# Output projections of an fp32 two-layer trunk: both token parts in one 512-column product, and the last down-projection token-major

## The chip, the cores and the metric

The kernel runs on one core of a Trainium2 chip. The metric is the device time of one execution in microseconds (us). Three runs of the kernel before gave 625.13, 625.70 and 626.88 us, median 625.7 us. The trace was taken on one further, profiled execution: its span, from the first to the last instruction, is 622.1 us.

## The reference

A batch of one, 256 tokens (S) of 1024 features (D), two layers, all float32. Layer 0 mixes tokens by attention, layer 1 by a gated short convolution; each is followed by a SwiGLU feed-forward with 2816 hidden features (D_FF). A conditioning vector c gives six rows of 1024 values for each layer (shift, scale and gate for the mixer, shift, scale and gate for the feed-forward):

```python
sc = jax.nn.silu(c)
for i in range(DEPTH):
    mod = sc @ w_ada[i] + b_ada[i]
    sh_m, sc_m, g_m, sh_f, sc_f, g_f = jnp.split(mod, 6, axis=-1)
    h = modulate(x, norm_mix[i], sh_m, sc_m)          # rmsnorm(x) * (1 + scale) + shift
    if i % N_MIXERS == 0:
        y = moba_attention(h, w_qkv[j], w_o[j], q_gain[j], k_gain[j])
    else:
        y = short_conv(h, w_in[j], conv_w[j], w_out[j])
    x = x + g_m[:, None, :] * y
    h = modulate(x, norm_ffn[i], sh_f, sc_f)
    x = x + g_f[:, None, :] * swiglu(h, w_gate_up[i], w_down[i])
return x
```

With 256 tokens there is one attention block, so the attention is plain causal attention in 8 heads of 128.

## The kernel before

**Products in parts.** A float32 operand is split into a high and a low part in TensorE's faster float32r format, and a product is three passes: high by high, high by low, low by high (mm3, L285 to L289). One pass is one TensorE instruction with a 128x128 stationary operand and 256 moving columns. A new stationary operand is loaded for each pass (the rows of PEld).

**Layout.** The residual x is held feature-major (xT: 128 features on the partitions, 8 tiles k, 256 tokens along). In most products the weights are stationary and the 256 tokens move, so that the result is feature-major again.

**The weight stream.** Weights and adaLN pieces come in chunks of up to 1 MB, all issued on SP's queue (load, L82 to L86) in the order of their use, into five buffers. A weight chunk (wf) is split into wh on ScalarE (L98) and wl on VectorE (L99), in two halves, into three buffers each. An adaLN piece (wa) is multiplied and summed on VectorE (L114, L116). A chunk's buffer is free again, and the next load can be issued, when its last reader on VectorE is done. What VectorE and ScalarE do, and in which order, is set by a scheduler that fills each engine's list from the order in which the program asks for the chunks (get, produce).

**Output projections.** out_proj (L406 to L431) does w_o of the attention (tiles op_o), w_out of the convolution (op_co), and w_down of both layers (op_d). It makes 2 tiles of 128 output features out of a column block of 256, over 8 k-steps for w_o and w_out and 22 for w_down: 64, 64, 176 and 176 steps (tile, k) of three passes. At the end of a tile, residual (L404) adds gate times product to xT in one VectorE instruction, and Norm.take prepares the next norm: a square and a scaled high part on ScalarE (L359, L373), the low part on VectorE (L374), a sum of squares on POOL (L364, L367). At its fifth tile (k == 4) it also writes the shift columns (L380, L381).

**After an output projection** comes raw_gemm (L437): the first two chunks of the next layer part are multiplied with the un-normed x (tiles raw_f, raw_m), and the norm's own sums over partitions (ms_n, L387 and L388) run in their midst, with POOL's sum and the last tile's square as operands.

**The last gate.** The gate of layer 1's feed-forward (part 5 of its adaLN) is summed over the partitions as 24 one-column bf16 products (mod_ps, L151) of three bf16 parts (L126, L127), right ahead of the last down-projection.

**The end.** store (L826 to L836) turns each finished tile of xT back to tokens: two 128x128 transposes by ident into out_ps (L828), a copy on ScalarE (L832), and a DMA on SP (L834, L836). The first six tiles' transposes run between products of the last down-projection, those of the last two after it.

## Time and profile before

| | us |
|---|---|
| three runs, median (lowest to highest) | 625.7 (625.13 to 626.88) |
| profiled execution: span, first to last instruction | 622.1 |
| profiled execution: its own time | not given beside the span; the median lies 3.6 above the span |
| PE busy | 609.7 (98%) |
| PEld busy | 595.8 (96%) |
| DVE busy | 473.6 (76%) |
| ACT busy | 323.1 (52%) |
| DMA moved | 156.07 MB, mean 251 GB/s |
| TensorE's granted clock over the span | 0.999 of full speed |

PE is TensorE's products, PEld its weight loads, DVE VectorE, ACT ScalarE, POOL GpSimd, SP SyncE (which issues the DMAs). Products overlap in the array, and a product's end is modelled, so a row's duration is longer than what the product costs. What one costs in a row of products is the distance from its start to the start of the next. Lines (L289) are lines of the kernel.

### The profile page before, as it was taken

Reading aid. Unit: us, or ns where it says so; the run is one execution under the profiler, and the core shown is the slowest. Engines: PE = TensorE matmul, PEld = TensorE weight load, DVE = VectorE, ACT = ScalarE, POOL = GpSimd, SP = SyncE. Lnnn points to the kernel's source line nnn. Section 1 sums busy time; section 2 is a strip of 40 time slices with the busy share of each in tenths; the row PEclk is TensorE's granted clock in tenths of the full one; section 3 lists DMA queues with packets and bytes.
Section 4 is the critical chain, followed back from the end, with each engine's and each line's share of the span. In section 5 each row is a group of like instructions: output and inputs, shape, how many; then the busy total and the mean of one; then the engine's idle time right before and its main releaser. Section 6 shows DMA issues by size and latency. Waiting matters only on the chain.

```text
span 622.1 us, 12512 instructions
## 1 busy us (share of the span) xinstructions
PE 609.7 (98%) x5291; PEld 595.8 (96%) x5291; DVE 473.6 (76%) x668; ACT 323.1 (52%) x518; POOL 19.2 (3%) x26
## 2 busy tenths in 40 slices
PE   7999999999999999999999999999999999999997
PEld 5789999999999999999999999998999999999997
DVE  5567999989989899979888989658976467644440
ACT  5335977466655455535355745545744435533330
POOL 0000000020000000000110000012000000000000
PEclk9999999999999999999999999999999999999999
DMA  9999999966699999798998497646388677655200
GB/s 271 329 331 354 385 370 335 303 219 223 210 323 322 347 333 335 257 318 303 319 302 278 133 304 241 210 138 205 108 299 271 201 225 235 204 188 178 94 18 17
DMA packets 127455, 156.07 MB, mean 251 GB/s; under 512 B 2822, under 2 KB 114856, under 8 KB 127400
## 3 DMA queue, kind: packets, MB, share of 16 engines
q1 hardware_dynamic: 127400, 155.28, 75.6%
q8 instruction: 41, 0.67, 0.5%
q14 instruction: 14, 0.11, 0.1%
HBM read 154.22 MB, written 1.05 MB: 250 GB/s over the span
## 4 chain that ended last, share of the span: by engine, by line
PE 88%; DMA 3%; DVE 3%; issue 3%; ACT 1%; SPq 0%; POOLq 0%; POOL 0%; ACTq 0%
PE pu L289 7%; PE pu L288 7%; PE op_d L287 7%; PE pu L287 7%; PE op_d L289 7%; PE op_d L288 7%; PE pg L289 6%; PE pg L288 6%; PE pg L287 6%; DMA wa<-in_w_ada_dram 2%; DMA wf_qk<-in_w_qkv_dram 1%; PE pv L287 1%; PE pb L288 1%; PE pv L289 1%; PE pb L287 1%
## 5 line engine op out<-in xcount | busy, mean ns | idle before, releaser
L116 DVE SCALAR_TENSOR_TENSOR acc<-wa,sc,acc 128x1024 f32<-128x1024 f32 x70 | 89.8, 1283 | 8.8 <-DMA wa<-in_w_ada_dram 7.5
L98 ACT ACTIVATE wh_d<-wf_d 128x1024 fp32r<-128x1024 f32 (+1 forms) x48 | 45.5, 981 | 69.7 <-issue 47.2
L99 DVE TENSOR_TENSOR wl_d<-wf_d,wh_d 128x1024 fp32r<-128x1024 f32 (+1 forms) x48 | 53.6, 1144 | 30.7 <-ACT wh_d L98 30.5
L98 ACT ACTIVATE wh_u<-wf_u 128x1024 fp32r<-128x1024 f32 x44 | 44.3, 1051 | 45.3 <-issue 34.5
L98 ACT ACTIVATE wh_g<-wf_g 128x1024 fp32r<-128x1024 f32 x44 | 45.5, 1050 | 40.7 <-issue 40.7
L99 DVE TENSOR_TENSOR wl_u<-wf_u,wh_u 128x1024 fp32r<-128x1024 f32 x44 | 52.7, 1233 | 14.0 <-ACT wh_u L98 14.0
L99 DVE TENSOR_TENSOR wl_g<-wf_g,wh_g 128x1024 fp32r<-128x1024 f32 x44 | 54.5, 1245 | 2.1 <-ACT wh_g L98 2.0
L287 PE MATMUL op_d<-a1h,wh_d 128*128 128x256 f32 x176 | 50.3, 286 | 0.0
L287 PE MATMUL op_d<-a0h,wh_d 128*128 128x256 f32 x176 | 50.2, 285 | 0.0
L289 PE MATMUL op_d<-a1h,wl_d 128*128 128x256 f32 x176 | 50.0, 284 | 0.0
L289 PE MATMUL op_d<-a0h,wl_d 128*128 128x256 f32 x176 | 50.0, 284 | 0.0
L288 PE MATMUL op_d<-a1l,wh_d 128*128 128x256 f32 x176 | 49.6, 282 | 0.0
L288 PE MATMUL op_d<-a0l,wh_d 128*128 128x256 f32 x176 | 49.5, 281 | 0.0
L289 PE MATMUL pg<-f1h,wl_g 128*128 128x256 f32 x160 | 44.8, 280 | 0.0
L289 PE MATMUL pu<-f1h,wl_u 128*128 128x256 f32 x160 | 44.8, 280 | 0.0
L287 PE MATMUL pg<-f1h,wh_g 128*128 128x256 f32 x160 | 44.6, 279 | 0.0
L288 PE MATMUL pg<-f1l,wh_g 128*128 128x256 f32 x160 | 44.6, 279 | 0.0
L287 PE MATMUL pu<-f1h,wh_u 128*128 128x256 f32 x160 | 44.6, 279 | 0.0
L288 PE MATMUL pu<-f1l,wh_u 128*128 128x256 f32 x160 | 44.6, 279 | 0.0
L287 PE MATMUL pg<-f0h,wh_g 128*128 128x256 f32 x160 | 44.5, 278 | 0.0
L289 PE MATMUL pg<-f0h,wl_g 128*128 128x256 f32 x160 | 44.4, 278 | 0.0
L289 PE MATMUL pu<-f0h,wl_u 128*128 128x256 f32 x160 | 44.4, 278 | 0.0
(315 smaller groups left out, 2103.6 us busy)
## 6 DMA issues: line engine op xcount, KB each, us to landing
wa<-in_w_ada_dram SPq DMA_DIRECT2D x40, 1024.0 KB, 6.1
wf_g<-in_w_gate_up_dram SPq DMA_DIRECT2D x22, 1024.0 KB, 6.6
wf_u<-in_w_gate_up_dram SPq DMA_DIRECT2D x22, 1024.0 KB, 7.5
wf_d<-in_w_down_dram SPq DMA_DIRECT2D x16, 1024.0 KB, 6.3
wa<-in_w_ada_dram SPq DMA_DIRECT2D x16, 512.0 KB, 7.1
wf_d<-in_w_down_dram SPq DMA_DIRECT2D x8, 768.0 KB, 5.7
wf_qk<-in_w_qkv_dram SPq DMA_DIRECT2D x8, 512.0 KB, 8.1
wf_v<-in_w_qkv_dram SPq DMA_DIRECT2D x4, 1024.0 KB, 7.5
```

The lines of the kernel that those rows point to most:

```text
L98: nc.scalar.activation(wh[:, a:b], wf[:, a:b], AF.Copy)
L99: nc.vector.tensor_sub(wl[:, a:b], wf[:, a:b], wh[:, a:b].bitcast(F32))
L116: nc.vector.scalar_tensor_tensor(acc, w[:, kk], sc[:, k:k + 1], acc, op0=ALU.mult, op1=ALU.add)
L287: nc.tensor.matmul(ps, ah, bh, start=first, stop=False, skip_group_check=True)
L288: nc.tensor.matmul(ps, ah, bl, start=False, stop=False, skip_group_check=True)
L289: nc.tensor.matmul(ps, al, bh, start=False, stop=last, skip_group_check=True)
```

## The change

1. **Pairs are one tile.** new_pair and wide_pair return one tile [128, 2, nk, 256] with the high part at index 0 and the low part at 1, so that both parts of one k lie in one access pattern.
2. **Output projections** of w_o, w_out and layer 0's w_down use mm512 in place of mm3: one product of 512 moving columns (the weight's high part by [high, low]) and one of 256 (the weight's low part by high), into the two halves of a PSUM tile of 512 columns. A step (tile, k) has two instructions where it had three; the moving columns stay 768. residual adds the two halves in two VectorE instructions where it was one: 24 more of 128x256 in all, 8 at each of the three.
3. **The last down-projection** is token-major (tok_wide, project): 128 tokens of an activation are stationary and 512 weight columns move. Its chunks are 4 k-steps of 512 columns (rows of 2 KB) where they were 8 of 256. 264 products of 512 columns stand where 528 of 256 stood. The end is a multiplication by the gate and an addition of x on VectorE for each of four 128x512 results, and a DMA.
4. **The last gate as rows.** b_ada's row is read broadcast into 128 partitions by a DMA on SP, and gate_rows adds the sum over partitions, by two float32 products of 512 columns, in place of the 24 bf16 ones and the making of their parts.
5. **x to tokens early.** The transposes of x (16 of 128x128, and 4 copies on ScalarE) are made in layer 1's feed-forward, after its second to fifth pair of chunks (to_tokens), where 16 of the result stood in and after the last down-projection.

The core of the diff:

```diff
     def new_pair(tag, name, nk):
-        return (act.tile([P, nk, S], F32R, tag=tag + "h", name=name + "h"),
-                act.tile([P, nk, S], F32R, tag=tag + "l", name=name + "l"))
+        return act.tile([P, 2, nk, S], F32R, tag=tag, name=name)
...
+    def mm512(ps, lhs, both, first, last):
+
+        ah, al = lhs
+        nc.tensor.matmul(ps, ah, both, start=first, stop=False, skip_group_check=True)
+        nc.tensor.matmul(ps[:, 1], al, both[:, 0], start=False, stop=last, skip_group_check=True)
+
     def residual(ps, l, gate, k):
-        nc.vector.scalar_tensor_tensor(xT[:, k], ps, mcol(l, gate, k), xT[:, k], op0=ALU.mult, op1=ALU.add)
+        for n in range(2):
+            nc.vector.scalar_tensor_tensor(xT[:, k], ps[:, n], mcol(l, gate, k), xT[:, k], op0=ALU.mult, op1=ALU.add)
...
-                    mm3(pss[j, o], (wh[:, k, cs], wl[:, k, cs]), (xs[0][:, base + k], xs[1][:, base + k]),
-                        base + k == 0, base + k == total - 1)
+                    mm512(pss[j, o], (wh[:, k, cs], wl[:, k, cs]), xs[:, :, base + k],
+                          base + k == 0, base + k == total - 1)
...
+    def gate_rows(acc):
+
+        for n in range(2):
+            cs = slice(n * 2 * CW, (n + 1) * 2 * CW)
+            ps = ps_misc(f"gate_ps_{n}")
+            nc.tensor.matmul(ps, one.to_broadcast([P, P]), acc[:, cs], start=True, stop=True)
+            nc.vector.tensor_add(last["gate"][:, cs], last["gate"][:, cs], ps)
...
+    WIDE = 2 * CW
+    DOWN = ((0, 4), (4, 4), (8, 4), (12, 4), (16, 4), (20, 2))
...
+        if l == DEPTH - 1:
+            for j in range(2):
+                for i, (a, n) in enumerate(DOWN):
+                    dn.append(w(("d", l, j, i), w_down[l][a * P:(a + n) * P, j * WIDE:(j + 1) * WIDE], n))
+            return gu, dn
...
+    def tok_wide(pss, keys, xs, between={}, final=False):
+
+        total, base = sum(nk for _, nk in keys), 0
+        for i, (key, nk) in enumerate(keys):
+            wh, wl = get(key)
+            steps = [(k, t) for k in range(nk) for t in range(2)]
+            if final and i == len(keys) - 1:
+                steps.sort(key=lambda s: s[1])
+            seen = set()
+            for k, t in steps:
+                if k not in seen:
+                    seen.add(k)
+                    for fn, *args in between.get(base + k, ()):
+                        fn(*args)
+                ts = slice(t * P, (t + 1) * P)
+                mm3(pss[t], (xs[:, 0, base + k, ts], xs[:, 1, base + k, ts]), (wh[:, k], wl[:, k]),
+                    base + k == 0, base + k == total - 1)
+            base += nk
...
+                if l == DEPTH - 1 and j < 5:
+                    last["turn"](j - 1)
...
-    def store(k):
-        ps = ps_misc(f"out_ps_{k}")
-        for t in range(2):
-            nc.tensor.transpose(ps[:, t * P:(t + 1) * P], xT[:, k, t * P:(t + 1) * P], ident)
...
+    def store(j, t, cs, ps):
+        y = tmp.tile([P, WIDE], F32, tag="s", name=f"y_{j}_{t}")
+        nc.vector.tensor_mul(y, ps, last["gate"][:, cs])
+        nc.vector.tensor_add(y, y, last["x"][:, t, cs])
+        nc.sync.dma_start(of[:, t, cs], y)
...
+    nc.sync.dma_start(last["gate"], b_ada[DEPTH - 1:, G_F * D:].to_broadcast([P, D]))
+
+    def to_tokens(n):
+        pt = ps_misc(f"xt_{n}")
+        for o in range(2):
+            for t in range(2):
+                nc.tensor.transpose(pt[:, t * S + o * P:][:, :P], xT[:, 2 * n + o, t * P:(t + 1) * P], ident)
+        nc.scalar.activation(last["x"][:, :, n * S:(n + 1) * S], pt.rearrange("p (t f) -> p t f", t=2), AF.Copy)
```

**TensorE at the start of layer 0's down-projection.** Before, each step (tile, k) is three rows of 256 columns; wh_d and wl_d are the weight's high and low part, a0h and a0l the activation's:

```order
2079 L287 MATMUL op_d_0_0_3387<-a0h,wh_d_0_0_3271 128x256
2080 L288 MATMUL op_d_0_0_3387<-a0l,wh_d_0_0_3271 128x256
2081 L289 MATMUL op_d_0_0_3387<-a0h,wl_d_0_0_3272 128x256
2082 L287 MATMUL op_d_0_1_3388<-a0h,wh_d_0_0_3271 128x256
2083 L288 MATMUL op_d_0_1_3388<-a0l,wh_d_0_0_3271 128x256
2084 L289 MATMUL op_d_0_1_3388<-a0h,wl_d_0_0_3272 128x256
```

Now the same place, where a_1534 is the activation's pair in one tile:

```order
2014 L432 MATMUL op_d_0_0_3324<-a_1534,wh_d_0_0_3208 128x512
2015 L433 MATMUL op_d_0_0_3324<-a_1534,wl_d_0_0_3209 128x256
2016 L432 MATMUL op_d_0_1_3325<-a_1534,wh_d_0_0_3208 128x512
2017 L433 MATMUL op_d_0_1_3325<-a_1534,wl_d_0_0_3209 128x256
2018 L432 MATMUL op_d_0_0_3324<-a_1534,wh_d_0_0_3208 128x512
2019 L433 MATMUL op_d_0_0_3324<-a_1534,wl_d_0_0_3209 128x256
```

The two passes over wh are one row now, and each tile's step has one row fewer.

**VectorE from w_o to the first feed-forward chunk.** Before; xT with L404 is the residual, a0l with L374 the low part of the next operand, L381 the shift columns, wl_u and wl_g the split of the coming chunks:

```order
199 L404 SCALAR_TENSOR_TENSOR xT<-op_o_2_1_1728,mod,xT 128x256
200 L99 TENSOR_TENSOR wl_u_0_1815<-wf_u_0_1812,wh_u_0_1814 128x1024
201 L374 SCALAR_TENSOR_TENSOR a0l<-xT,mod,a0h 128x256
202 L99 TENSOR_TENSOR wl_u_0_1815<-wf_u_0_1812,wh_u_0_1814 128x1024
203 L381 TENSOR_TENSOR a0l<-mod,a0h 128x8x2
204 L404 SCALAR_TENSOR_TENSOR xT<-op_o_3_0_1810,mod,xT 128x256
205 L374 SCALAR_TENSOR_TENSOR a0l<-xT,mod,a0h 128x256
206 L404 SCALAR_TENSOR_TENSOR xT<-op_o_3_1_1811,mod,xT 128x256
207 L374 SCALAR_TENSOR_TENSOR a0l<-xT,mod,a0h 128x256
208 L99 TENSOR_TENSOR wl_g_1_1888<-wf_g_1_1885,wh_g_1_1887 128x1024
209 L374 SCALAR_TENSOR_TENSOR a0l<-xT,mod,a0h 128x256
```

Now:

```order
207 L103 TENSOR_TENSOR wl_u_0_1768<-wf_u_0_1765,wh_u_0_1767 128x1024
208 L400 SCALAR_TENSOR_TENSOR a_1534<-xT,mod,a_1534 128x256
209 L437 SCALAR_TENSOR_TENSOR xT<-op_o_2_1_1695,mod,xT 128x256
210 L407 TENSOR_TENSOR a_1534<-mod,a_1534 128x8x2
211 L103 TENSOR_TENSOR wl_u_0_1768<-wf_u_0_1765,wh_u_0_1767 128x1024
212 L437 SCALAR_TENSOR_TENSOR xT<-op_o_3_0_1763,mod,xT 128x256
213 L400 SCALAR_TENSOR_TENSOR a_1534<-xT,mod,a_1534 128x256
214 L437 SCALAR_TENSOR_TENSOR xT<-op_o_3_0_1763,mod,xT 128x256
215 L437 SCALAR_TENSOR_TENSOR xT<-op_o_3_1_1764,mod,xT 128x256
216 L103 TENSOR_TENSOR wl_g_1_1826<-wf_g_1_1823,wh_g_1_1825 128x1024
217 L400 SCALAR_TENSOR_TENSOR a_1534<-xT,mod,a_1534 128x256
218 L437 SCALAR_TENSOR_TENSOR xT<-op_o_3_1_1764,mod,xT 128x256
```

Each residual tile has two rows (L437). The shift columns (L407) stand ahead of the second half of wl_u, and half of wl_g_1 stands ahead of the last residual row.

**TensorE at the end of layer 1's gate and up products.** Now the two gate products stand where 24 rows of mod_ps (L151, 128x1) stood, and then the first token-major products (y_0 and y_1 are the two halves of the tokens; the activation pair a_4795 is stationary):

```order
4283 L312 MATMUL pu_10_6348<-f_5131,wh_u_10_6287 128x256
4284 L142 MATMUL gate_ps_6473<-acc_5_5542,one 128x512
4285 L142 MATMUL gate_ps_6476<-acc_5_5542,one 128x512
4286 L310 MATMUL y_0_6471<-wh_d_0_0_6355,a_4795 128x512
4287 L311 MATMUL y_0_6471<-wl_d_0_0_6356,a_4795 128x512
4288 L312 MATMUL y_0_6471<-wh_d_0_0_6355,a_4795 128x512
4289 L310 MATMUL y_1_6472<-wh_d_0_0_6355,a_4795 128x512
```

All rows of the last down-projection have 512 columns, and no transposes stand among them.

## Rows read from the trace of the kernel before

**Rows 1.** The page: busy time of each engine, and the chain that ended last.

```profile
PE 609.7 (98%) x5291; PEld 595.8 (96%) x5291; DVE 473.6 (76%) x668; ACT 323.1 (52%) x518; POOL 19.2 (3%) x26
...
PE 88%; DMA 3%; DVE 3%; issue 3%; ACT 1%; SPq 0%; POOLq 0%; POOL 0%; ACTq 0%
```

**Rows 2.** Waits of PE over the span: line, releaser, us, times, longest.

```profile
PE raw_f L288 <- DVE a0l L381: 1.1, 1, 1.1
PE ms_n L387 <- POOL ss_n L367: 1.0, 1, 1.0
```

**Rows 3.** Busy time by stage: w_o, layer 0's down-projection, w_out, layer 1's.

```profile
core 0: us, PE busy (x) PEld busy (x) DVE busy (x) ACT busy (x) POOL busy (x), PEclk, DMA share, GB/s
112.10:139.40 27.30, 27.30 (x223) 25.99 (x222) 24.19 (x38) 15.76 (x30) 4.11 (x4) 1.00 0.79 255
266.40:330.60 64.20, 64.20 (x568) 64.16 (x565) 55.88 (x60) 30.92 (x42) 4.65 (x5) 1.00 0.92 309
401.00:424.10 23.10, 23.10 (x207) 23.10 (x204) 15.60 (x21) 12.40 (x21) 4.84 (x5) 1.00 0.49 155
552.30:617.60 65.30, 65.30 (x558) 65.05 (x554) 26.11 (x30) 20.35 (x27) 0.00 (x0) 1.00 0.29 96
```

**Rows 4.** Timeline of PE in layer 0's down-projection: start, duration, engine, line.

```profile
299.24 0.28 PE L288 MATMUL op_d<-a0l,wh_d 128*128 128x256 f32 x1
...
300.44 0.29 PE L289 MATMUL op_d<-a0h,wl_d 128*128 128x256 f32 x1
```

**Rows 5.** Timeline of PE at a head's attention output (x2: two passes).

```profile
113.88 0.59 PE L737 MATMUL po<-vp 128*128 128x256 f32 x2
114.31 0.39 PE L738 MATMUL po<-vp 128*128 128x128 f32 x2
```

**Rows 6.** Timeline of PE at a transpose.

```profile
96.10 0.27 PE L729 MATMUL prt<-ident,pr 128*128 128x128 f32 x1
96.21 0.60 PE L737 MATMUL po<-vp 128*128 128x256 f32 x2
```

**Rows 7.** Timeline of DVE from w_o to the feed-forward (fp32r: float32r).

```profile
137.61 1.21 DVE L99 TENSOR_TENSOR wl_u<-wf_u,wh_u 128x1024 fp32r<-128x1024 f32 x1
...
141.30 0.17 DVE L381 TENSOR_TENSOR a0l<-mod,a0h 128x16 fp32r<-128x16 f32 x1
141.38 0.47 DVE L404 SCALAR_TENSOR_TENSOR xT<-op_o,mod,xT 128x256 f32<-128x256 f32 x1
...
142.44 0.48 DVE L404 SCALAR_TENSOR_TENSOR xT<-op_o,mod,xT 128x256 f32<-128x256 f32 x1
```

**Rows 8.** Waits of SP's queue in 264 to 331 us.

```profile
SPq L85 <- DVE wl_d L99: 23.9, 8, 4.5
```

**Rows 9.** Timeline of PE at the last gate's sums.

```profile
551.94 0.75 PE L151 MATMUL mod_ps<-one_b,part 128*128 128x1 bf16 x24
552.55 0.36 PE L287 MATMUL op_d<-a1h,wh_d 128*128 128x256 f32 x1
```

**Rows 10.** Timeline of PE, DVE and ACT at the end.

```profile
617.36 0.28 PE L289 MATMUL op_d<-a1h,wl_d 128*128 128x256 f32 x1
...
618.75 0.38 ACT L832 ACTIVATE osb<-out_ps 128x256 f32<-128x256 f32 x1 [0.43 <-PE out_ps L828]
```

**Rows 11.** The product of two 128x512 tiles, one in PSUM, on DVE.

```profile
L814 DVE TENSOR_TENSOR z<-y,pb x4: 680/686/692, 353.8 to 400.8; 128x512 f32<-128x512 f32 x4
```

**Rows 12.** Timeline of PE in both layers' gate and up products.

```profile
199.36 0.75 PE L151 MATMUL mod_ps<-one_b,part 128*128 128x1 bf16 x24
...
225.10 0.28 PE L289 MATMUL pg<-f0h,wl_g 128*128 128x256 f32 x1
...
227.26 0.28 PE L287 MATMUL pu<-f0h,wh_u 128*128 128x256 f32 x1
...
460.07 0.28 PE L287 MATMUL pu<-f1h,wh_u 128*128 128x256 f32 x1
...
462.31 0.28 PE L288 MATMUL pg<-f1l,wh_g 128*128 128x256 f32 x1
```

More of the change, by code (lines that the diff above doesn't have):

```diff
@@ L103, in trunk_kernel @@
     acc_of = {}
-    late, gets = [], [0]
+    late, gets, last = [], [0], {}
     def ada_piece(l, part, i):
@@ L118, in ada_piece @@
             return
+        if (l, part) == (DEPTH - 1, G_F):
+            late.append((gets[0], lambda: gate_rows(acc)))
+            return
         if l == 0 and part != G_F:
@@ L291, in feat_gemm @@
     def feat_gemm(parts, xs, nk):
-        xh, xl = xs
+        xh, xl = halves(xs)
         for k in range(nk):
@@ L421, in out_proj @@
                         last = k
-                        for fn, *args in between.get(k, ()):
+                        for fn, *args in between.get(base + k, ()):
                             fn(*args)
@@ L481, in ffn @@
                 nc.vector.tensor_mul(a, s, pu)
-            split(av, slice(2 * j, 2 * j + 2), a, f"{l}_{j}")
-        out_proj([[(("d", l, j, i), n) for i, n in enumerate((8, 8, 6))] for j in range(4)], av, l, G_F, done)
+            split(av, slice(2 * j, 2 * j + 2), a)
+        project(l, av, [], done)
     def mod_sums(w, name):
```

97 lines of the change are left out of this document (58 added, 39 removed).

## The prediction

> **What bounds the kernel now.** I read the busy times first. TensorE is busy for 98% of the span and its weight loads for 96%; VectorE, at 76%, has room on the mean [rows 1]. The chain that ended last says the same: 88% of it is TensorE [rows 1]. The waits of TensorE come next, and two of them touch the change: 1.1 us at the start of the first feed-forward, until VectorE has written the shift columns, and 1.0 us ahead of the norm's sums after w_out, until POOL has its sum [rows 2]. So the time is the number of TensorE's products times their spacing, and then what VectorE does at the junctions. The table by stage shows where VectorE has no room: in layer 0's down-projection it is busy for 55.9 of 64.2 us and DMA for 92%, while in layer 1's it is busy for 26.1 of 65.3 us [rows 3].
>
> The spacing itself is in the timeline of products. In layer 0's down-projection ten 256-column products follow from 299.24 to 300.44 us, 120 ns each, so a step (tile, k) of three costs 360 ns [rows 4]. The trace has no 512-column product in float32r. The nearest is the attention output in float32, which goes through the array in two passes for 256 columns: from 113.88 to 114.31 us, 0.43 us, or 215 ns a pass with a weight load in between [rows 5].
>
> **The change part by part.**
>
> *The 512-column product.* I take 215 ns for it, by the attention rows, and 120 ns for the 256-column one beside it: 335 ns a step, 25 ns less than before. The bounds are wide: two 256-column products at the closest spacing the trace has, 114 ns, make 228 ns [rows 12], or at 120 ns 240 ns and no saving at all [rows 4]; at best 215 and 114 make 329 ns, 31 ns less. I stay with 25, since the attention rows are the only ones in which a pass is that long.
>
> The row of 120 ns for 256 columns and that of 215 ns for a double pass are set against a rule: the Trainium skill, "TensorE: Matmul & The Clock Gate", section "Back-to-back issue gap", gives columns over 2.4 GHz plus 2.5 ns for one product alone, 109 and 216 ns. The trace agrees on the long one and is 11 ns above it on the short one. By that rule alone two short products would cost only 2.5 ns more than a long one, and the change would give 0.4 us in layer 0's down-projection, where the rows give 4.4.
>
> *w_o (64 steps).* TensorE saves 64 x 25 ns = 1.6 us. But this junction is VectorE's: TensorE already waits there for the shift columns, written at 141.30 us [rows 2, 7]. Eight residual rows are added, one of them costing 0.40 us (0.47 less the overlap with the next). Six of them stand ahead of the shift columns, 2.4 us. The shift columns now stand ahead of half of wl_u, which is worth 1.2 us (the 1.21 of wl_u's half [rows 7]), and three more products of the high part are issued before TensorE needs them. What is then late is the last residual row, at 142.44 us before [rows 7]: behind half of wl_g now, and POOL's sum and the norm's sums on TensorE wait for it. My value is nothing gained, nothing lost. The bounds are 1.6 gained, if VectorE had slack, and 3.8 lost (8 x 0.40, and 0.6 for the part of wl_g).
>
> *Layer 0's down-projection (176 steps).* 176 x 25 ns = 4.4 us on TensorE. VectorE gets 3.2 us more, 59.1 us where only 59.8 would be left: 99% busy. SP's queue waits there for buffers that VectorE's split of the weights frees, 23.9 us in eight waits [rows 8], so that a late split also delays the next load. A lead of some chunks and the sums of the adaLN pieces can give way for a while. I take 1.0 us off, 3.4 us gained. The bounds: 176 x 31 ns = 5.5 us gained with full cover; and, if VectorE cannot exceed the 87% it has now, 59.1 / 0.87 = 67.9 us, 3.7 lost.
>
> *w_out (64 steps).* 1.6 us on TensorE. VectorE is busy for 15.6 of 23.1 us [rows 3], so the earlier tiles' residuals are covered. The second rows of the last two tiles lie ahead of POOL's sum, for which TensorE already waits [rows 2]: 0.8 us. 0.8 us gained; bounds 1.6 gained and 2.4 lost (8 x 0.40 less 0.8).
>
> *The last down-projection.* 528 x 120 ns = 63.4 us become 264 x 215 ns = 56.8 us: 6.6 saved. Bounds: 0, and 6.6, since I know no shorter pass. Against it stand: the gate's two float32 products, twice two passes of 512 columns at two cycles each by the attention rows (0.43 us for 256 columns), 0.88 us each and 1.76 in all, in place of 0.61 (551.94 to 552.55) [rows 9]: 1.15 lost. The transposes: the stage lasts from 552.55 to 617.48 us, 64.9, so the 12 transposes in its midst cost 1.5 us, 0.13 each [rows 9, 10]; a transpose alone is spaced 0.11 us [rows 6]. 16 now go into layer 1's feed-forward, 2.1 us: 0.6 lost. At the end, 1.65 us pass from the last product's end to ScalarE's last copy (617.48 to 619.13) [rows 10]. Now a multiplication and an addition of 128x512 follow, 0.69 us each by the convolution's row [rows 11], 1.4 us, and a DMA of 256 KB instead of 128; the two even out. The broadcast of the gate adds 0.5 MB to SP's queue in a stage without waits of TensorE, and VectorE gets rid of 4 instructions for the parts; both are covered. Together 6.6 - 1.15 - 0.6 = 4.9 gained. The new chunks have fewer, longer rows; with DMA busy for 29% of the stage [rows 3] that is worth nothing either way.
>
> **Sum.** 0 + 3.4 + 0.8 + 4.9 = 9.1 us. The profiled execution would go from a span of 622.1 to 613.0 us. The median of the runs lies 3.6 us above that span, and nothing in the change touches what lies around it: 625.7 - 9.1 = 616.6 us.
>
> **The rivals.**
>
> *Faster spacing in layer 1's feed-forward: 613.0 us.* In layer 0's feed-forward the gate and up products are 113.7 ns apart (19 of them from 225.10 to 227.26), after a burst of one-column products at 199.36 had broken their row; in layer 1's, unbroken, they are 117.9 ns apart (19 from 460.07 to 462.31) [rows 12]. The new transposes break that row too. 864 products (nine pairs of chunks, 96 each) by 4.2 ns would give another 3.6 us. Against it: the burst at 551.94 us [rows 9] did not bring the down-projection behind it below 120 ns.
>
> *VectorE and the stream take the gain away: 620.8 us.* If the stages of layer 0 and w_out end when VectorE ends, only the last down-projection's 4.9 us are left. For it speak the 99% above and the wait at w_o; against it that TensorE did not wait once inside layer 0's down-projection, and that VectorE's work can be put off.
>
> *The long product costs two short ones: 623.2 us.* At 228 ns it saves 12 ns a step: 2.1 - 1.0 = 1.1 us in layer 0's down-projection, nothing at w_out (0.8 less the 0.8 of the two last tiles), and in the last one 63.4 - 264 x 228 ns = 3.2, less 1.75, 1.4. Together 2.5 us. The attention rows speak against it.
>
> *Slower: 630 us.* The 24 residual rows sit in chains that VectorE already sets. Where they are not covered, w_o loses 3.8, layer 0's down-projection 3.7 and w_out 2.4 us, 9.9 in all, against 4.9 gained: 5 us slower. It decides against the change once the three lose over 4.9 us together. For it speaks that VectorE is in the releasing place in both waits at w_o; against it the 32% of free VectorE time at w_out.
>
> *Much faster.* If each 512-column product came 131 ns after the one ahead, the last down-projection would save 63.4 - 34.6 = 28.8 us and the 304 steps 109 ns each, 33 us: some 565 us. The attention rows, with 215 ns, deny it. That figure is what the Trainium skill, "TensorE: Matmul & The Clock Gate", section "Back-to-back issue gap", states for a sustained stream of loads and products; no run here shows it.
>
> **How the numbers follow.** The forecast has 0.47 (its own range 614.5 to 619), the faster spacing 0.22, VectorE taking the gain 0.19, the long product without gain 0.07, slower 0.04, much faster 0.01. A measurement of this kernel can tell 0.3%, about 1.9 us, from no change. The range from 611 to 621.5 us takes in the first three with their bounds and leaves out less than 0.2. Faster by over 0.3%: 0.92; all but a few hundredths of the cases that end below 623.8. Within 0.3%: 0.04, from the edges of the second and third rival. Slower: 0.04.
>
> **What would show it.** In the profile after, the products with 512 columns follow each other after 215 ns in the last down-projection (57 us long), and a step in layer 0's takes 335 ns. VectorE's busy share in layer 0's down-projection is near 0.97. TensorE's waits for the shift columns and for the norm's sums stay at 1 to 3 us. The feed-forward of layer 1 is longer by 2 us if its spacing stays at 118 ns, and shorter by 1.5 if it falls to 114. The forecast is wrong if TensorE waits for wl_d or wh_d in layer 0's down-projection, or if the 512-column product comes out at 228 ns or more.

## The result and the profile after

The kernel after takes 631.81 us (629.66 to 632.15, 4 runs) against 625.64 us before: 1.0095 times the time, 95% interval 1.0073 to 1.0117. It is 6 us slower where 9 us less were forecast. The profiled execution has a span of 630.3 us, 8.2 more than before.

The page of after, busy time and chain, against [rows 1]:

```profile
PE 614.6 (98%) x4703; PEld 575.0 (91%) x4703; DVE 482.2 (77%) x691; ACT 320.2 (51%) x512; POOL 20.2 (3%) x26
...
PE 87%; DVE 5%; DMA 4%; issue 2%; ACT 1%; POOLq 0%; POOL 0%; SPq 0%; ACTq 0%; DVEq 0%
```

TensorE has 588 instructions less and is busy for 4.9 us more. VectorE's share of the chain went from 3% to 5%. Two things are to be looked for: what a product costs, and where VectorE now ends a wait.

Waits of TensorE in after, against [rows 2]:

```profile
PE raw_f L310 <- ACT a L406: 2.6, 2, 1.5
PE ms_n L413 <- POOL ss_n L393: 2.1, 2, 1.1
PE raw_f L311 <- DVE a L407: 0.8, 1, 0.8
PE op_co L432 <- DVE xT L437: 0.6, 2, 0.4
```

The junctions after w_o and w_out cost 5.5 us of waits where they cost 2.4 before (2.1 in [rows 2], and 0.3 for the second layer's shift columns), and TensorE waits 0.6 us inside w_out for a residual, which it never did before.

Busy time by stage in after (columns as in [rows 3]): w_o, layer 0's feed-forward and down-projection, w_out, the norm's chunks behind it, layer 1's feed-forward and down-projection:

```profile
113.10:141.70 28.60, 26.91 (x161) 22.71 (x159) 26.31 (x44) 15.66 (x30) 4.53 (x4) 1.00 0.77 246
155.80:273.00 117.20, 117.20 (x1027) 116.80 (x1026) 105.31 (x119) 62.44 (x78) 0.00 (x0) 1.00 0.87 293
273.00:336.00 63.00, 63.00 (x406) 54.83 (x403) 58.17 (x66) 30.97 (x42) 4.49 (x5) 1.00 0.86 291
406.30:431.40 25.10, 23.27 (x144) 19.74 (x140) 17.87 (x28) 13.20 (x21) 4.77 (x5) 1.00 0.47 155
431.40:448.00 16.60, 14.58 (x105) 14.17 (x106) 11.81 (x25) 6.99 (x16) 2.41 (x2) 0.90 0.54 178
448.00:564.90 116.90, 116.90 (x983) 116.42 (x982) 75.65 (x84) 57.41 (x72) 0.00 (x0) 1.00 0.66 217
564.90:625.00 60.10, 60.10 (x265) 49.40 (x265) 26.37 (x29) 18.00 (x21) 0.00 (x0) 1.00 0.28 96
```

And in before the three of these stages that [rows 3] leaves out, layer 0's feed-forward, the chunks behind w_out, layer 1's feed-forward:

```profile
153.90:266.40 112.50, 112.50 (x1026) 112.39 (x1025) 101.71 (x111) 61.26 (x75) 0.00 (x0) 1.00 0.89 301
424.10:438.60 14.50, 13.14 (x108) 12.72 (x107) 11.62 (x24) 7.58 (x16) 2.23 (x2) 1.00 0.57 189
438.60:552.30 113.70, 113.70 (x978) 113.66 (x977) 77.19 (x86) 56.95 (x70) 0.00 (x0) 1.00 0.68 221
```

Stage by stage, after less before, from one product's start to the next stage's: w_o +0.9 us, layer 0's feed-forward +4.6, its down-projection -1.7, the convolution +0.4, w_out +2.1, the chunks behind it +2.0, layer 1's feed-forward +3.3, the last down-projection to the end of the span -4.4. The start (1.7 longer up to the first q product, 0.7 won back until w_o) differed by as much between the traces of after and of runs that share its start (13.1 to 15.3 us up to the first q product), so I leave it out. The largest loss is in the feed-forward of layer 0, which the change did not touch: same products, same columns, no wait of TensorE.

In the last 6 us of w_out VectorE has no pause:

```profile
425.40:431.40 6.00, 4.80 (x28) 3.96 (x26) 6.00 (x10) 3.27 (x6) 2.28 (x3) 1.00 0.36 122
```

Timelines of after, start and duration: three steps of mm512, seven gaps of the token-major products, nine of the feed-forward's:

```profile
299.82 0.40 PE L432 MATMUL op_d<-a,wh_d 128*128 128x512 f32 x1
...
300.88 0.40 PE L432 MATMUL op_d<-a,wh_d 128*128 128x512 f32 x1
```

```profile
589.84 0.39 PE L312 MATMUL y<-wh_d,a 128*128 128x512 f32 x1
...
591.42 0.39 PE L310 MATMUL y<-wh_d,a 128*128 128x512 f32 x1
```

```profile
207.76 0.28 PE L312 MATMUL pg<-f,wl_g 128*128 128x256 f32 x1
...
208.84 0.28 PE L312 MATMUL pg<-f,wl_g 128*128 128x256 f32 x1
```

A step is 1.06 / 3 = 353 ns (forecast 335, before 360; 347 in the second half of the stage), a 512-column product 1.58 / 7 = 226 ns (forecast 215), and a feed-forward product 1.08 / 9 = 120 ns, where before had 114 in the same stretch [rows 12], the one between two bursts of one-column products.

In the chunks behind w_out the clock falls. Granted clock in after, and two products in it:

```profile
437.60:440.50 2.90, 2.90 (x16) 2.90 (x17) 2.08 (x4) 0.26 (x1) 0.00 (x0) 0.56 0.09 28
```

```profile
438.21 0.42 PE L312 MATMUL raw_f<-a,wl_g 128*128 128x258 f32 x1
438.43 0.42 PE L310 MATMUL raw_f<-a,wh_g 128*128 128x258 f32 x1
```

Behind waits for the shift columns and for POOL's sum, the mean granted clock is 0.56, near 1.2 of 2.4 GHz, and products come 215 ns apart. That is most of the stage's 2.0 us.

### The profile page after: what moved, and what is told of

The parts are those of the page before. It is cut to its first block, busy times and chain, and to the rows that moved or that the text cites. A ratio compares the mean times of both kernels' runs of the same rounds, so it can differ in the third digit from the quotient of the medians.

```text
span 630.3 us, 11361 instructions
## 1 busy us (share of the span) xinstructions
PE 614.6 (98%) x4703; PEld 575.0 (91%) x4703; DVE 482.2 (77%) x691; ACT 320.2 (51%) x512; POOL 20.2 (3%) x26
## 4 chain that ended last, share of the span: by engine, by line
PE 87%; DVE 5%; DMA 4%; issue 2%; ACT 1%; POOLq 0%; POOL 0%; SPq 0%; ACTq 0%; DVEq 0%
PE pu L312 7%; PE pu L310 7%; PE pu L311 7%; PE op_d L432 7%; PE pg L310 6%; PE pg L311 6%; PE pg L312 6%; PE op_d L433 3%; PE y L311 3%; PE y L310 3%; PE y L312 3%; DMA wf_qk<-in_w_qkv_dram 1%; PE pv L310 1%; DMA wa<-in_w_ada_dram 1%; DVE xT L437 1%
## 5 line engine op out<-in xcount | busy, mean ns | idle before, releaser
L310 PE MATMUL pg<-f,wh_g 128*128 128x256 f32 x320 | 90.7, 283 | 0.0
L312 PE MATMUL pu<-f,wl_u 128*128 128x256 f32 x320 | 90.5, 283 | 0.0
L312 PE MATMUL pg<-f,wl_g 128*128 128x256 f32 x320 | 90.4, 282 | 0.0
L311 PE MATMUL pg<-f,wh_g 128*128 128x256 f32 x320 | 90.3, 282 | 0.0
L310 PE MATMUL pu<-f,wh_u 128*128 128x256 f32 x320 | 90.2, 282 | 0.0
L311 PE MATMUL pu<-f,wh_u 128*128 128x256 f32 x320 | 90.2, 282 | 0.0
L103 DVE TENSOR_TENSOR wl_d<-wf_d,wh_d 128x1024 fp32r<-128x1024 f32 (+2 forms) x48 | 53.8, 1153 | 28.6 <-ACT wh_d L102 28.6
L432 PE MATMUL op_d<-a,wh_d 128*128 128x512 f32 x176 | 61.9, 397 | 0.0
L312 PEld LDWEIGHTS pu<-f,wl_u 128*128 128x128 f32 x320 | 60.3, 188 | 0.2 <-DVE wl_u L103 0.2
L311 PEld LDWEIGHTS pg<-f,wh_g 128*128 128x128 f32 x320 | 60.3, 189 | 0.1
L310 PEld LDWEIGHTS pu<-f,wh_u 128*128 128x128 f32 x320 | 60.4, 189 | 0.0
L310 PEld LDWEIGHTS pg<-f,wh_g 128*128 128x128 f32 x320 | 60.4, 189 | 0.0
L311 PEld LDWEIGHTS pu<-f,wh_u 128*128 128x128 f32 x320 | 60.3, 188 | 0.0
L312 PEld LDWEIGHTS pg<-f,wl_g 128*128 128x128 f32 x320 | 60.3, 188 | 0.0
```

What stands on the lines that cost most here:

```text
L103: nc.vector.tensor_sub(wl[:, a:b], wf[:, a:b], wh[:, a:b].bitcast(F32))
L310: nc.tensor.matmul(ps, ah, bh, start=first, stop=False, skip_group_check=True)
L311: nc.tensor.matmul(ps, ah, bl, start=False, stop=False, skip_group_check=True)
L312: nc.tensor.matmul(ps, al, bh, start=False, stop=last, skip_group_check=True)
L432: nc.tensor.matmul(ps, ah, both, start=first, stop=False, skip_group_check=True)
```

## The experiments

A ratio below is to the kernel before, run beside the same runs; its median lay between 623.8 and 625.6 us, so two runs from different sets are better compared by their ratios than by their times.

**Is it the place of the tiles?** In the built programs, tiles start 32 or 96 bytes past a multiple of 128 in SBUF. The weights stand at 96. The feed-forward's operand stood at 32 in before, and the merged tiles put it at 96 in after. Counted from the weights, modulo 256 bytes, that is a distance of 64 in before and of 128 in after.

a_al64 (after) and b_al64 (before) move weights, activations and temporaries alike, by 32 bytes:

```diff
+    wpad = wpool.tile([P, 8], F32, name="wpad")
```

> The kernel after, with an unused tile of 32 bytes per partition ahead of the weight buffers, so that all weight buffers, activations and temporaries start 32 bytes later in SBUF: at multiples of 128 bytes instead of 96 past one. Nothing else changes. Theory A (place): the spacing of products depends on where the rows of their operands start; 120 ns is nine eighths of 106.7 (256 columns at 2.4 GHz), 226.7 is seventeen sixteenths of 213.3, as if a row that starts off a grid cost one piece more. Then 256-column products fall from 119-121 to 107-112 ns and those of 512 from 227-230 to 213-218, and the time falls by 25 to 40 us to 592-607 us, unless VectorE or DMA bind first. Theory B (order): the spacing is a pattern that the queue falls into after each break in the row of products, by the order of instructions; place is nothing. Then 631.8 us within 0.3%, and 119-121 and 227 ns stay.

> The kernel before with the same unused 32 bytes ahead of the weight buffers. Theory A (place): products at 107-113 ns instead of 113-120, 592-607 us. Theory B (order): 625.6 us within 0.3%.

Measured: 628.85 us (1.0066 of before, 1.0042 to 1.0091) and 625.07 (1.0009, 0.9995 to 1.0023). Neither theory as put: no product fell to 107 ns, so a grid that rows must start on isn't it. The first gained 2 to 3 us (by ratio and by median), 1.2 of them in the chunks behind w_out (15.3 us for 16.5), with the feed-forwards at 118.7 ns. The second has the time of before, but not all its stages: layer 0's feed-forward took 115.1 us for 112.5, at 117.8 ns throughout, where before has 117.8 up to the first burst of one-column products and 113.3 behind it.

a_act64 and b_act64 move the activations alone, by 64 bytes, and leave the weights:

```diff
+    apad = act.tile([P, 16], F32, name="apad")
```

> The kernel after with an unused tile of 64 bytes ahead of the activations alone: they start 64 bytes later (32 past a multiple of 128 instead of 96), weights stay where they are (96 past). The feed-forward operand then starts at the same place on a grid of 128 bytes as in the kernel before. Theory A (place, on a grid of 128): the feed-forwards' spacing goes from 119-121 back to 113-118 ns, and the time falls by 4 to 6 us to about 626-628 us. Theory B (order): 631.8 us within 0.3% and the same spacing.

> The kernel before with the same 64 bytes ahead of the activations: the feed-forward operand, 32 past a multiple of 128 bytes, comes to 96 past one, as in the kernel after. Theory A (place, on a grid of 128): the feed-forward's 113-118 ns become 118.7-121 and the time rises by 4 to 6 us to 630-632 us; the down-projections, whose operand goes from 96 to 32, may fall from 120 ns and give up to 4 us back. Theory B (order): 625.6 us within 0.3%.

Measured: 625.26 us (1.0001, 0.9985 to 1.0017) and 629.09 (1.0068, 1.005 to 1.0087). One pad takes the loss off after, and the same pad makes before slower by 0.7%; the directions are theory A's, and both times lie up to 1 us below its ranges. The two feed-forwards of after with it, and layer 0's of before with it:

```profile
155.30:270.80 115.50, 115.50 (x1025) 115.10 (x1024) 104.78 (x119) 62.36 (x78) 0.00 (x0) 1.00 0.88 297
444.00:556.40 112.40, 112.40 (x983) 111.88 (x982) 75.48 (x85) 57.64 (x72) 0.00 (x0) 1.00 0.69 225
```

```profile
154.60:270.50 115.90, 115.90 (x1026) 115.77 (x1025) 102.19 (x111) 60.80 (x75) 0.00 (x0) 1.00 0.88 296
```

With the first pair of runs, the distance between the moving and the stationary operand counts for most of it, and not either's own place. It is not all: in after the pad gave layer 0's feed-forward 1.6 of its 4.6 us back, and layer 1's 4.6 where 3.3 had been lost, since its products came 113.3 ns apart from the first transposes on, faster than in before. (Modulo 256 the pad puts the operand of after at 192, not at the 64 of before.)

**TensorE alone.** bench1 and bench2 issue nothing but rows of products at chosen distances (d) between stationary and moving operand; they leave the computation out. The feed-forward's row is:

```diff
+            for k in range(8):
+                for o in range(2):
+                    cs = slice(o * P, (o + 1) * P)
+                    for n, (a, b) in enumerate(((wh, xh), (wh, xl), (wl, xh))):
+                        nc.tensor.matmul(ps[:, o], a[:, k, cs], b[:, k], start=k == 0 and o == 0 and n == 0,
+                                         stop=k == 7 and n == 2, skip_group_check=True)
```

> Leaves the whole computation out and writes zeros: TensorE alone, with rows of products as in the kernel, each row with the moving operand at another distance from the stationary one. Names: f0064x is the feed-forward's pattern (wh by xh, wh by xl, wl by xh, 256 columns) with xh 64 bytes past wh modulo 8192; y0064x the token-major pattern of 512 columns, b0064x the pair of 512 and 256 columns; four transposes part the rows. Theory A (distance modulo 128 bytes): f0000x 118.7 to 121 ns, f0064x 113 or 118, and the same at distances 128, 256, 512, 2048 as at 0; y0000x 226.7, y0064x 233; b0000x 173 to 177 ns mean of the two. Other distances (16, 32, 48) are not known, and may be better. Theory B' (what moves the spacing is traffic of other engines or of DMA, which differs in place with the tiles): without any other engine all rows have one spacing, 107 to 114 ns.

Rows of bench1 (start, duration of the row of 96 or 48 products; the number in the name is the distance in bytes):

```profile
24.77 11.76 PE L72 MATMUL f0000x<-buf 128*128 128x256 f32 x96
...
70.33 11.47 PE L72 MATMUL f0064x<-buf 128*128 128x256 f32 x96
...
104.67 11.04 PE L72 MATMUL f0112x<-buf 128*128 128x256 f32 x96
115.55 11.55 PE L72 MATMUL f0128x<-buf 128*128 128x256 f32 x96
```

```profile
297.45 11.07 PE L87 MATMUL y0000x<-buf 128*128 128x512 f32 x48
...
341.63 11.36 PE L87 MATMUL y0064x<-buf 128*128 128x512 f32 x48
```

Behind the first few products, from the starts: 120.0 ns at 0, 117.8 at 64, 113.3 at 112, 118.6 at 128; 512 columns 226.7 ns at 0 and 16, 232 to 234 at the others; mm512's steps 349 to 356 ns. The pattern is there with every other engine idle, so theory B' falls. A 512-column product costs two 256-column ones at the best place.

> Leaves the whole computation out and writes zeros: TensorE alone, as the first row bench, with finer distances. There the feed-forward's pattern ran at 120.0 ns at distance 0, 117.8 at 64 and 113.3 at 112, and the 512-column pattern at 226.7 at 0 and 16 and at 232 to 234 else. Theory A (distance modulo 128 bytes): f0112x is at 113.3 again, whatever number of transposes stands ahead (names with m1, m2, m3, m5); 64 stays at 117.8. Theory A2 (the distance only allows several patterns, and the break ahead chooses): f0112 and f0064 change between 113.3 and 118 with the number of transposes. For the 512-column product neither theory gives less than 226.7, twice 113.3, and none of these rows comes to 215.

bench2: 113.3 to 113.6 ns at 112 and 117.8 at 64 with every number of transposes ahead: A, not A2, for TensorE alone. Other distances were no better (116.7 at 8, 130 at 104), and no row of 512-column products was below 226.6 ns on the mean. The good distance is that of the feed-forward's pattern, with the weights stationary. In the token-major pattern of 256 columns (n: the activation is stationary, the weights move) it is another, 113.3 ns at 64 and 120.0 at 112:

```profile
333.56 11.05 PE L127 MATMUL n0064x<-buf 128*128 128x256 f32 x96
...
367.24 11.68 PE L127 MATMUL n0112x<-buf 128*128 128x256 f32 x96
```

**The 512-column product and the doubled residual.** d_mm3 is after with mm3 and one residual row in out_proj; d_2res adds to d_mm3 a second row that adds nothing:

```diff
-                    mm512(pss[j, o], (wh[:, k, cs], wl[:, k, cs]), xs[:, :, base + k],
-                          base + k == 0, base + k == total - 1)
+                    mm3(pss[j, o][:, 0], (wh[:, k, cs], wl[:, k, cs]), (xs[:, 0, base + k], xs[:, 1, base + k]),
+                        base + k == 0, base + k == total - 1)
...
-        for n in range(2):
+        for n in range(1):
```

```diff
+    zero = const.tile([P, 1], F32, name="zero")
+    nc.vector.memset(zero, 0.0)
...
-        for n in range(1):
-            nc.vector.scalar_tensor_tensor(xT[:, k], ps[:, n], mcol(l, gate, k), xT[:, k], op0=ALU.mult, op1=ALU.add)
+        for g in (mcol(l, gate, k), zero):
+            nc.vector.scalar_tensor_tensor(xT[:, k], ps[:, 0], g, xT[:, k], op0=ALU.mult, op1=ALU.add)
```

> The kernel after with three products of 256 columns (mm3) and one residual row in the output projections of w_o, w_out and layer 0's down-projection; the pair tiles, the token-major last down-projection, the gate rows and the early transposes stay. If the 512-column product brings what its trace shows (351 for 360 ns a step, 3.0 us over 304 steps) and the doubled residual rows cost more than that at the junctions after w_o and w_out (0.9 and 4 us longer in the trace of after), this is faster than after, by 1 to 4 us: 628 to 631 us. If the 512-column product helps on balance, it is slower than after: 633 to 636 us.

> The kernel after with mm3 in the output projections, as in the run before it with one residual row (627.35 us), and a second residual row a tile that adds the same product times a column of zeros: the doubled VectorE rows without the 512-column products. If the doubled rows are what lengthened the stages after w_o and w_out (0.9 and 2.4 us, and 0.3 to 1.8 in the products after it), this run shows 3 to 5 us more than with one row, 630 to 632 us, with the w_out stage at 24.5 to 25.5 us instead of 22.7. If it is the 512-column products themselves (their weights' or operands' waits), it stays at 627 to 628 us.

Measured: 627.35 us (1.0045, 1.003 to 1.006) and 631.67 (1.0119, 1.0089 to 1.0148). w_o, w_out and the chunks behind w_out in d_mm3, then in d_2res:

```profile
113.80:141.50 27.70, 27.59 (x223) 26.07 (x221) 24.59 (x39) 16.00 (x31) 4.64 (x5) 1.00 0.79 257
406.30:429.00 22.70, 22.70 (x206) 22.70 (x203) 15.35 (x21) 12.40 (x21) 4.60 (x5) 1.00 0.48 153
429.00:443.70 14.70, 13.17 (x108) 12.75 (x107) 11.81 (x24) 7.60 (x16) 2.46 (x2) 1.00 0.69 229
```

```profile
111.40:140.80 29.40, 28.05 (x224) 26.19 (x222) 26.29 (x45) 15.91 (x31) 4.53 (x4) 1.00 0.72 243
407.20:432.60 25.40, 23.98 (x208) 23.36 (x205) 17.88 (x28) 12.29 (x20) 4.76 (x5) 1.00 0.47 153
432.60:447.90 15.30, 14.26 (x105) 14.05 (x106) 11.84 (x25) 7.75 (x17) 2.42 (x2) 0.89 0.61 194
```

24 residual rows, 9.6 us of VectorE's time at 0.40 each, cost 4.3 us of the kernel's. In the traces w_o is 1.7 us longer and w_out 2.7, both at a full clock; at their ends the chain that ended last runs on VectorE. The chunks behind them are 1.8 longer, with the clock fallen in d_2res and not in d_mm3, and the time up to w_o is 2.4 shorter. So a part of the 4.3 us is the clock: the four executions of d_2res had mean granted clocks of 0.994 to 0.997, eight of the ten of d_mm3 0.999 or 1.0.

Between d_2res and after, which adds the 512-column product to that, there is nothing to be measured in the time. The trace has 1.7 us less in layer 0's down-projection (63.0 for 64.7 us) and 0.9 more in the feed-forward ahead of it.

**The distance, used.** b_112 moves every moving activation of before to 112 bytes past the weights modulo 128, by offsets inside their tiles:

```diff
-        return (act.tile([P, nk, S], F32R, tag=tag + "h", name=name + "h"),
-                act.tile([P, nk, S], F32R, tag=tag + "l", name=name + "l"))
+        off = {"h": 12, "a": 28}[tag]
+        return tuple(act.tile([P, nk * S + 32], F32R, tag=tag + p, name=name + p)[:, off:off + nk * S].rearrange(
+            "p (k s) -> p k s", s=S) for p in "hl")
...
-        flat = [act.tile([P, RAW], F32R, tag="z" + p, name=name + p) for p in "hl"]
+        flat = [act.tile([P, RAW + 32], F32R, tag="z" + p, name=name + p)[:, o:o + RAW] for p, o in (("h", 28), ("l", 12))]
```

> The kernel before with its activations moved inside their tiles so that both parts of each start 112 bytes past the weights modulo 128 (feature operands were 64 past, the down-projections' and w_o's 0 or 64). Nothing else changes. Theory A (distance): feed-forward, convolution and output projections run near 113.3 ns instead of 117.8 and 120, some 4,000 products by 4 to 6 ns, 16 to 24 us less where VectorE and the stream keep up: 602 to 612 us. Theory A2 (the break ahead chooses): 113.3 in some stretches only, 614 to 624 us. Theory B (order alone): 625.6 us.

620.18 us (0.9927, 0.9903 to 0.9952), in the range of theory A2, not of A. The down-projections came to 113.6 ns; the feed-forwards stayed at 117.8. w1 puts the feed-forward's two parts 8192 bytes apart, in one tile; w3, its edit given against w1 in the last lines, gives the down-projection's low tile 128 bytes more room, which moves the high part behind it:

```diff
+        if tag == "h":
+            t = act.tile([P, 2 * nk * S + 32], F32R, tag="h", name=name)[:, 12:12 + 2 * nk * S]
+            t = t.rearrange("p (n k s) -> p n k s", n=2, s=S)
+            return t[:, 0], t[:, 1]
...
-        return tuple(act.tile([P, nk * S + 32], F32R, tag=tag + p, name=name + p)[:, 28:28 + nk * S].rearrange(
-            "p (k s) -> p k s", s=S) for p in "hl")
+        return tuple(act.tile([P, nk * S + room], F32R, tag=tag + p, name=name + p)[:, 28:28 + nk * S].rearrange(
+            "p (k s) -> p k s", s=S) for p, room in (("h", 32), ("l", 64)))
```

> The kernel before with activations 112 bytes past the weights modulo 128 as in the run before (620.18 us), but the two parts of the feed-forward operand in one tile, the low part 8192 bytes after the high one, as in the rows of TensorE alone that ran at 113.3 ns (they were 8320 apart). If that distance is what kept the feed-forward at 117.8 ns at 112, the feed-forwards and the convolution come to 113.3 ns, 2,400 products by 4.5 ns, and the time to 609 to 613 us. If the distance modulo 128 and the break ahead are all that counts, 617 to 622 us.

> As the run before it (616.55 us), with the down-projections' low part moved by 128 bytes, so that the distance between high and low part is a multiple of 256 bytes there too (it was 128 off one). In the two runs at 112 bytes past the weights, products ran at 113.4 ns where that distance was a multiple of 256 (down-projections of the one, feed-forwards of the other) and at 117.8 where it was not (the other way round). If that holds, both down-projections come to 113.5 ns and stages of 61.4 and 63.5 us, the feed-forwards stay at 113.4, and the time is 611 to 613.5 us. If the two had only changed places by the break ahead, 616 to 619 us.

w1: 616.55 us (0.9864, 0.9844 to 0.9883), in neither of its ranges, feed-forwards at 113.4, but the down-projections at 117.8. w3: 620.33 (0.9933, 0.9912 to 0.9953): down-projections and w_out at 113.5, feed-forwards at 117.1. Its expectation, 611 to 613.5, missed, since the theory was incomplete: by the built addresses, each stage at 113.5 had both parts at 112 modulo 256, and each at 117.1 to 117.8 had one or both at 240. w4 puts all of them at 112 modulo 256 (its edit to w3):

```diff
-            t = act.tile([P, 2 * nk * S + 32], F32R, tag="h", name=name)[:, 12:12 + 2 * nk * S]
+            t = act.tile([P, 2 * nk * S + 64], F32R, tag="h", name=name)[:, 44:44 + 2 * nk * S]
...
-        flat = [act.tile([P, RAW + 32], F32R, tag="z" + p, name=name + p)[:, o:o + RAW] for p, o in (("h", 28), ("l", 12))]
+        flat = [act.tile([P, RAW + (32 if p == "h" else 64)], F32R, tag="z" + p, name=name + p)[:, o:o + RAW] for p, o in (("h", 28), ("l", 44))]
```

> The kernel before with every activation that moves against weights (feed-forward, output projections, down-projections; both parts) 112 bytes past the weights modulo 256, where the runs so far had 112 or 240. In them, products ran at 113.4 to 113.9 ns where both parts stood at 112 modulo 256 and at 117.1 to 117.8 where one or both stood at 240. If modulo 256 is the rule, all stages but the norm's chunks come to 113.5 ns: feed-forwards of 111.0 and 109.5 us, down-projections of 61.4 and 63.5, 609 to 613 us. If not, 616 us or more.

613.11 us (611.04 to 614.8), 0.9809 of before (0.9785 to 0.9833). Layer 0's feed-forward and down-projection, then layer 1's:

```profile
156.30:267.30 111.00, 111.00 (x1027) 110.89 (x1026) 101.45 (x110) 61.66 (x74) 0.00 (x0) 1.00 0.89 303
267.30:328.70 61.40, 61.40 (x583) 61.33 (x581) 56.09 (x62) 31.64 (x44) 4.69 (x5) 1.00 0.94 316
...
436.40:545.80 109.40, 109.40 (x979) 109.36 (x978) 76.94 (x86) 56.99 (x70) 0.00 (x0) 1.00 0.71 229
545.80:609.40 63.60, 62.93 (x560) 62.21 (x556) 26.59 (x31) 20.94 (x29) 0.00 (x0) 1.00 0.31 100
```

All four are as expected, to 0.1 us; the time is 0.1 us above the range. No version was faster by more than can be measured, and none of the change is in it.

**What is left of the change.** w2 and w4t keep the token-major half alone: d_mm3 with the pairs moved inside their tiles (offsets in floats of w4t; w2 has 16 for m and f):

```diff
+    OFFS = {'m0': 28, 'f0': 28, 'm1': 28, 'f1': 28, 'a0': 28, 'a1': 0}
...
-        return act.tile([P, 2, nk, S], F32R, tag=tag, name=name)
+        off = OFFS[name]
+        t = act.tile([P, 2 * nk * S + 32], F32R, tag=tag, name=name)[:, off:off + 2 * nk * S]
+        return t.rearrange("p (n k s) -> p n k s", n=2, s=S)
```

> The token-major half of the change alone, with the places chosen: mm3 and one residual row in the output projections, token-major last down-projection at distance 0 (226.7 ns), the feed-forward's operand at distance 64 as in the kernel before, layer 0's down-projection at 112. If the place explains what d_mm3 (627.35 us) lost, its feed-forwards and convolution return to 113-118 ns (-4 to -1 us), layer 0's down-projection to 113.5 (-3.4): 619 to 623 us. If pairs in one tile or the token-major half itself cost the time, it stays at 624 us or more.

> The token-major half of the change alone (mm3 and one residual row in the output projections) with the feed-forward's and layer 0's down-projection's operands at 112 modulo 256, and the last down-projection's at 0, where 512 columns took 226.7 ns. At these places a 512-column product costs what two of 256 do. If modulo 256 is the rule, feed-forward of layer 0 111.0 us, down-projection 61.4; and against the run beside it the last down-projection stage is 1.6 us shorter (no transposes in it) while layer 1's feed-forward is 2.4 us longer (transposes, gate): 610 to 615 us, within 0.3% of it.

w2: 621.40 us (0.9954, 0.9938 to 0.9971), as expected. w4t: 613.46 (0.9824, 0.9802 to 0.9847), the same as w4 within what can be measured. Its last two stages, against the last two above:

```profile
433.80:545.80 112.00, 112.00 (x982) 111.51 (x982) 75.50 (x85) 57.59 (x72) 0.00 (x0) 1.00 0.69 225
545.80:607.70 61.90, 60.68 (x266) 49.55 (x264) 28.13 (x31) 17.99 (x21) 0.00 (x0) 1.00 0.28 97
```

1.7 us less down there, 2.6 more ahead of it. Where both kinds of product stand at their good distance, a 512-column product costs two of 256, and transposes and gate only changed places: the token-major form gained in after because its products at distance 0 take 226.7 ns, where two of 256 columns took 240.

That the whole times agree is in part luck. In w4t the operands of w_o and w_out stand at 128 and 192 by the built addresses, and it takes 3.4 us longer than w4 in w_o, the convolution and w_out together. In w4's trace the clock fell in the chunks behind w_o and w_out, which took 16.3 and 18.1 us; in w4t's it did not, and they took 14.1 and 14.4.

a_h64 undoes in after one thing, the place of the operand of the feed-forwards, the convolution and the q, k and v products (64 modulo 256 as in before, where after has 128), by the same edit with 64 floats of room and these offsets:

```diff
+    OFFS = {'m0': 48, 'f0': 48, 'm1': 48, 'f1': 48, 'a0': 0, 'a1': 0}
```

> The kernel after with only the feed-forward and convolution operand moved: 64 bytes past the weights modulo 256, as in the kernel before, where it is 128 in the kernel after. Everything else as in after, the 512-column products too. If the place of this operand made its feed-forwards slower, layer 0's goes from 117.2 us to between 115.1 and 112.5, the convolution from 57.6 to 57.15 and layer 1's feed-forward from 117.0 to 116.1: 626 to 630 us. If the pair tile or the order did it, 631 to 632 us.

627.31 us (1.0029, 1.001 to 1.0048), 4 us below after. Feed-forwards of 115.5 and 115.3 us, against 117.2 and 116.9:

```profile
154.60:270.10 115.50, 115.46 (x1025) 115.04 (x1024) 104.84 (x119) 62.67 (x79) 0.00 (x0) 1.00 0.88 300
445.00:560.30 115.30, 115.30 (x983) 114.82 (x982) 74.80 (x81) 57.47 (x72) 0.00 (x0) 1.00 0.67 220
```

So the place accounts for 1.6 of the 4.6 us in layer 0's feed-forward. Most of the rest is in before: 576 of its products ran at 113.3 ns, behind a burst of one-column products, and here all run at 117.8. In layer 1's feed-forward of a_h64 one can watch the spacing change. Each group of four transposes turns it over, from 117.8 to 113.3 ns and back; 20 gaps behind the first group, and 20 behind the second:

```profile
460.21 0.28 PE L311 MATMUL pg<-f,wh_g 128*128 128x256 f32 x1
...
462.48 0.28 PE L310 MATMUL pu<-f,wh_u 128*128 128x256 f32 x1
...
472.00 0.28 PE L311 MATMUL pg<-f,wh_g 128*128 128x256 f32 x1
...
474.36 0.28 PE L310 MATMUL pu<-f,wh_u 128*128 128x256 f32 x1
```

2.27 / 20 is 113.5 ns, 2.36 / 20 is 118. The third group brought 113.3 again and the fourth 117.8. At a distance of 128 the same transposes, in after, left the products at 118.5 to 118.7 ns.

## Why the prediction was wrong

- **The price of the 512-column product** was the first step to fail. I took 215 ns from the attention rows, whose operands are plain float32 in two passes; in float32r it takes 226.7 to 234 ns, with TensorE alone too. A step saved 6 to 13 ns rather than 25, and layer 0's down-projection 1.7 us, where the sum had 3.4. My own bound of 228, two closest short ones, was the right end. The sign of being wrong, 228 ns or more, was set too high: 226.7 already takes 3 of the 6.6 us in the last down-projection. The Trainium skill, "TensorE: Matmul & The Clock Gate", section "Back-to-back issue gap", has 109 and 216 ns for one product alone, and 131 ns for a sustained stream of 512 columns. The float32r rows here stayed at 113.3 and 226.6 or above on the mean, and none was near 131.
- **VectorE at the junctions.** "My value is nothing gained, nothing lost" for w_o and "0.8 us gained" for w_out failed: w_o lost 0.9 us, w_out and the chunks behind it 4.1, the latter partly by the clock. d_2res shows the rows as the cause, 4.3 us with what the clock took. That VectorE was free for 32% of w_out did not cover them: the mean says nothing about its last 6 us, in which VectorE had no pause. And [rows 2] has one wait at w_o, not the two of which the prediction speaks; the other is behind w_out, and POOL ends it.
- **The part that isn't in the forecast.** That merging the high and low tiles changes the place of an operand, and its distance to the weights, was in no term and no rival. a_h64 puts 4.1 us on it. I had seen 113.7 and 117.9 ns side by side [rows 12] and laid it to the burst of one-column products ahead, with a rival in which the new transposes bring 114 in layer 1. That was half of it. At a distance of 64 or 192, inside the kernel, the spacing did change at such breaks (before, a_h64, a_act64), but not at each (the same burst changed nothing in b_al64), and at the 128 to which the change moved the operand none brought 113. In the rows of TensorE alone, transposes change nothing. What decides at a break stays open.
- **The last down-projection** was forecast at 4.9 us gained, with its costs in the feed-forward. By stages it gained 4.4 less 3.3, of which 0.9 is the spacing (960 products by 0.9 ns): 2.0 net. 264 products at 226.7 ns make 59.8 us, not 56.8: the 3 us that are missing.
- **The rival of the slower side** had 630 us, near the 631.8, but by another sum: layer 0's down-projection did not lose 3.7 us (VectorE went to 92% there, and TensorE never waited), and the feed-forwards were not in it. It was right in one of three places, and that its number is near is luck. "The long product costs two short ones" had the right price and 623 us, with the junctions at nothing.

By stages, as forecast and as in the traces (gained, in us): w_o 0 and -0.9; layer 0's down-projection 3.4 and 1.7; w_out with the chunks behind it 0.8 and -4.1; the last down-projection with its costs 4.9 and 2.0; the spacing of products that the change did not touch, nothing and -5.9 (feed-forwards 4.6 and 0.9, convolution 0.4).

By runs, each by its ratio to before: of the 0.95% that after is slower, a_h64 takes 0.66 off, 4.1 us, and d_mm3, without the 512-column products and their residual rows, 0.50, 3.1 us (4.5 by the medians). The token-major half is left with a gain of 1 to 3 us, by difference only, if the two add up; each ratio is known to 0.15 to 0.3%.

## What to carry over

Before pricing a merged or wider instruction by a similar row, look whether the row's operand type is the same; between two candidates take the one in the same type, here two short products. An edit that changes sizes of tiles moves all tiles behind them: if products of an untouched stage change their spacing, compare start addresses first. And a doubled small instruction is to be priced at the point where its engine is waited for, by the last microseconds there, not by its mean share. Effects of 1 to 2 us are to be read between executions with the same granted clock.

## What the runs showed of the hardware

The spacing of float32r products depends on where the moving row starts relative to the stationary one. Feed-forward pattern, both parts at one distance modulo 256 bytes: 113.3 to 113.6 ns at 112; 117.1 at 240; 117.8 at 64 and 192 (113.3 as well in the kernel, behind some breaks in the row); 118.6 to 120.0 at 128; 120.0 at 0. With one part at 112 and the other at 240: 117.8. With 512 weight columns moving and the activation stationary, by the activation's distance from the weights: 226.7 at 0, 16 and 120, 231 to 234 at most others; with 256 weight columns moving, 113.3 at 64 and 117.8 to 120.0 at the seven others tried. Adding the same 32 bytes to all (b_al64) left 117.8 and 120.0 as they were, but took away the stretch at 113.3 that before had at 64. Why these distances are good stays open: no run looks inside.

In the chunks behind w_o and w_out, just behind waits of 1 to 2.4 us, the granted clock fell in some traces and not in others: to 0.56 in the stretch of after that is shown above, with products at 215 ns, and to 0.50 in w4 and a_h64. The length of the wait alone does not decide it. The clock fell in b_act64, whose longest such waits are 1.0 and 1.1 us as in before, in whose trace it did not fall; and a_act64 had waits as long as those of after with no fall (its mean granted clock, then its waits of TensorE):

```profile
core 0: 623.5 us, clock 1.000
...
PE raw_f L312 <- ACT a L408: 2.4, 2, 1.4
...
PE ms_n L415 <- POOL ss_n L395: 2.2, 2, 1.2
```

The kernel before shows what a lower clock costs. Of its 74 executions beside the experiments, 31 had a mean granted clock of 0.998 to 1.0 and took 623.6 to 624.3 us (one 625.1); 38 had 0.996 or 0.997 and took 625.0 to 625.8 (one 626.6); five had 0.994 and took 626.8 to 627.2. That is some 1.6 us for each step down, as much as several of the effects above. No run changed the wait alone. In w4 the chunks behind w_out took 18.1 us, where w4t at a full clock took 14.4, so a version of w4 without that wait and the fall would have some 3.6 us more to gain by this estimate; it was not tried.
